# A decoder layer with attention and state-space mixers: VectorE in place of GpSimd, attention's scaling on ScalarE, and the mixers' TensorE instructions ranked 30 places later

## The chip, the cores and the metric

The kernel runs on one core of a Trainium2 chip. The metric is device microseconds of one execution of the whole program. A core has five instruction streams that run side by side and wait for one another by semaphores: TensorE (PE in the profile; its weight loads, PEld, overlap its matmuls), VectorE (DVE), ScalarE (ACT), GpSimd (POOL) and SyncE (SP), which here issues nearly all DMAs. Each stream runs its own instructions in order. An instruction whose input is not there holds all that stand behind it on that engine.

## The reference

One layer of a hybrid decoder, for a prompt of 2048 tokens and for 8 single sample tokens that share its weights. All in fp32, model width 1024, feed-forward width 2816.

```python
h = rms_norm(x, norm1_w)
q, k, v, z, xbc, dt_raw = jnp.split(h @ w_in, SPLIT_IDX, axis=-1)
a = swa_prompt(q, k, v, attn_sinks, rel_bias)        # window 128, 8 heads of 64, 2 kv heads, sinks, bias
s_out, new_conv, new_h = ssm_mixer(z, xbc, dt_raw, conv_buf, h0, ...)   # conv, chunked scan of 128, gate, norm
x = x + jnp.concatenate([a, s_out], axis=-1) @ w_out
h2 = rms_norm(x, norm2_w)
x = x + (jax.nn.silu(h2 @ w_gate) * (h2 @ w_up)) @ w_down
return rms_norm(x, final_norm_w), new_k, new_v, new_conv, new_h
```

The samples do the same with a cache of keys, values, convolution rows and scan state. The kernel returns the outputs and the new caches.

## The kernel before

The tokens are columns, the features partitions. The 16 blocks of 128 tokens and the 8 samples go through in six groups: 2, 3, 3, 3, 3 blocks, and 2 blocks with the samples, so N, the columns of a matmul, is 256, 384 (four times) and 264.

**Split products.** To keep fp32 accuracy, each large product is three passes: both the weight and the activation are split into a hi part (a rounded copy) and a lo part (the value less hi), and `mm3` adds hi by hi, hi by lo and lo by hi. A projection (`proj`) of one unit of 128 outputs is 8 x 3 = 24 matmuls into one of four PSUM banks called psd. The mixers' matmuls and transposes use four others, psm.

**Weights.** `weight` (line 199) gives one half unit. The first uses of a weight load it raw into one of four `wraw` buffers (line 206, on SP), copy it to hi on ACT (207) and subtract on POOL and DVE in turn (lines 208 to 210) for lo. Two steps later the pair is stored to DRAM (214, on SP), at the first, second or third use of the weight, so that a third of the weights is kept at each of the first three groups. From then on the pair is loaded ready-made (203). Five `w2` buffers hold pairs. Loads and stores stand in one queue, SP's.

**Stages of a group.** X (`stage_x`, for the first group `stage_x0`): load, square (ACT), sum (`total`, POOL), reciprocal root (`rinv_b`: one matmul with ones, ACT, DVE) and scaling into hi and lo (`scaled`, lines 333 to 349, whose `low` takes POOL and DVE in turn). A, K, B: the projections of the convolution's inputs, keys and values, queries and gate, with the convolution on DVE and ACT. P: attention, block by block (`attention`, 532). Q: the scan (`ssd`, 704) and its norm. Y: the samples. S: the split of the mixed output (`low`, 919). O: the output projection, with squares and sums for the next norm (`norm_sum`, 950). H: the second norm. F: the feed-forward with `up`, `down`, and hidden parts split by `hid1` and `hid2` (1003 to 1010). Z: the last norm and the output.

**Attention**, in the parts touched: the keys' lo (line 554, POOL), scores on TensorE, a fused bias and maximum on DVE (568), exponentials on ACT (588), the reciprocal of the sum (593, DVE), the scaling of the probabilities by it, four instructions of 128x128 for each key head (603, POOL), transposes (608), hi and lo, a product with the triangle for hi (626, POOL) and for lo (628, DVE), and the product with the values. **The scan**, likewise: the decays are cut to size (738, eight instructions on DVE), and POOL makes the products at 742, 750 and 757.

**The order.** The stages are generators. `run(main, rest)` (1067) steps the main one, a projection at a time, then `tick()`, which issues what `later` has put off, and then a share of each of the others. So the mixers of group i+1 and the first norm of group i+2 are woven into the feed-forward of group i. The program's instructions are issued in this order, each with a rank one higher than the last, and a planner then lays out every engine's stream by the ranks and by its own times: of the instructions it takes to be ready on an engine, the lowest rank comes first. The streams are then fixed.

Of the kernel before, what the change touches and what calls it, by code (L numbers as in the profile page):

```python
# [17 lines left out]
P = 128  # L18
# [10 lines left out]
RH0 = 3  # L29
DM = 1024  # L30
KT = DM // P
NH = 8
# [37 lines left out]


@with_exitstack
def hymba(ctx: ExitStack, tc: tile.TileContext, I: dict, O: dict, groups):
# [26 lines left out]

    V, S, G, PE, SP = nc.vector, nc.scalar, nc.gpsimd, nc.tensor, nc.sync

# [96 lines left out]
    def weight(name, at, w=512):  # L199
        t = T([P, 1024], F32R, tag="w2", bufs=5)[:, :2 * w]  # L200
        hi, lo = t[:, :w], t[:, w:]
        if (name, at) in kept:
            SP.dma_start(t.bitcast(F32), kept[name, at])
            return hi, lo
        raw = T([P, 512], tag="wraw", bufs=4)[:, :w]
        SP.dma_start(raw, I[name][at] if name != "wd" else I[name][:, at:at + w])
        S.activation(hi, raw, AF.Copy)  # L207
        e = G if wn[0] % 2 else V
        wn[0] += 1
        e.tensor_tensor(lo, raw, hi.bitcast(F32), ALU.subtract)  # L210
        k = seen[name, at] = seen.get((name, at), len(seen) % 3) - 1
        if k < 0:
            d = kept[name, at] = DR([P, 2 * w], f"{name}{len(kept)}")
            later(2, lambda: SP.dma_start(d, t.bitcast(F32)))
        return hi, lo
# [65 lines left out]
    def stage_x0(g):  # L281
# [18 lines left out]
        for m in range(KT):  # L300
            G.tensor_tensor(xr[:, m, :N], xr[:, m, :N], xr[:, m, :N], ALU.mult)
            if m:
                V.tensor_tensor(xr[:, 0, :N] if m < KT - 1 else r, xr[:, 0, :N], xr[:, m, :N], ALU.add)
            if m % 4 == 3:
                yield
# [13 lines left out]

    def total(sq, t, N, e=G):  # L320
        e.tensor_tensor(sq[:, :N], sq[:, :N], t[:, :N], ALU.add)  # L321
# [11 lines left out]
    def scaled(x, c, r, N, pair, to):  # L333
# [119 lines left out]
    def stage_k(g):  # L453
# [16 lines left out]
        def rows():  # L470
# [8 lines left out]
            for i, src in enumerate((vf[:, 0:nb], vd[:, :nb])):  # L479
                src = src.rearrange("p b (v c) -> p b v c", v=2)  # L480
                S.activation(vs[:, i, :nb, :, 0:64], src, AF.Copy)
                G.tensor_tensor(vs[:, i, :nb, :, 64:P], src, vs[:, i, :nb, :, 0:64].bitcast(F32), ALU.subtract)
            if last:
# [48 lines left out]
    def attention(g, b):  # L532
# [17 lines left out]
        for kv in range(2):  # L550
            a, o = half[kv], half[1 - kv]
            V.tensor_tensor(qs[o, 4 * kv:4 * kv + 4, :], qT[a, :, tk], qs[a, 4 * kv:4 * kv + 4, :].bitcast(F32), ALU.subtract)
            for r in (a, o):
                G.tensor_tensor(kl[r, kv, :W], kT[a, (b + k0) * P:(b + 2) * P], kh[a, kv, :W].bitcast(F32), ALU.subtract)
        yield
# [44 lines left out]
        def scale(kv):  # L600
            for r in range(4):
                h = kv * 4 + r
                G.tensor_scalar(sc[kv][:, r, 0:P], sc[kv][:, r, 0:P], rd[:, h:h + 1], 1.0, ALU.mult, ALU.mult)

# [11 lines left out]
        def finish(kv):  # L616
# [7 lines left out]
            if not first:  # L624
                own = part(), part()
                G.tensor_tensor(as4(own[0]), as4(f32(ph)), tri4, ALU.mult)
                yield
# [26 lines left out]
    def stage_q(g):  # L654
# [17 lines left out]
        for s0, s1 in ss:  # L672
            G.tensor_tensor(s0[:, :N], s0[:, :N], s1[:, :N], ALU.add)
        yield
# [29 lines left out]
    def ssd(g, b):  # L704
# [36 lines left out]
        xdd = T([P, NH, 64], tag="m2", bufs=M2)  # L741
        G.tensor_tensor(xdd, xdt, sm[:, 1, :].unsqueeze(2).broadcast_to([P, NH, 64]), ALU.mult)
        yo = PS("m")
# [5 lines left out]
        V.tensor_tensor(t1, yo.rearrange("p (a i) -> p a i", a=4), ecs, ALU.mult)  # L749
        G.tensor_tensor(state, state, sm[:, 0, :].unsqueeze(2).broadcast_to([P, NH, 64]), ALU.mult)  # L750
        st = PS("m")
# [3 lines left out]
        for q in range(2):  # L755
            e = csb[:, 4 * q:4 * q + 4, :]
            G.tensor_tensor(e, e, cb[:, q, :].unsqueeze(1).broadcast_to([P, 4, P]), ALU.mult)
        V.tensor_tensor(state, st.rearrange("p (h d) -> p h d", h=NH), state, ALU.add)
# [14 lines left out]
    def stage_y(g):  # L773
# [111 lines left out]
        for i in range(NS):  # L885
# [6 lines left out]
            V.tensor_tensor(f4(xb), bb(bcb, 0), f4(dx[:, 1, :, i:i + 1].broadcast_to([P, 4, P])), ALU.mult)  # L892
            G.tensor_tensor(h, h, dx[:, 0, :, i:i + 1].broadcast_to([P, 4, P]), ALU.mult)
            yield
            G.tensor_tensor(h, h, xb, ALU.add)
            SP.dma_start(O["nss"][:, i], h)
# [15 lines left out]
    def stage_s(g):  # L912
# [6 lines left out]
        def low(t):  # L919
            e = G if t % 2 else V  # L920
            e.tensor_tensor(mix[1][:, t, :N], src[t], mix[0][:, t, :N].bitcast(F32), ALU.subtract)
# [28 lines left out]
    def norm_sum(g, x1, sq, m, N, n=1):  # L950
# [6 lines left out]
        def second():  # L957
            if m:
                total(sq, t[0], N, V if g is gs[-1] and n == 0 else G)
            g["nsq"] = g.get("nsq", 0) + 1  # L960
# [15 lines left out]
    def stage_f(g):  # L976
# [30 lines left out]
        def hid2(f, t, hh, hl):  # L1007
            e = G if f % 2 else V
            e.tensor_tensor(hl[:, 0, :N], t[:, :N], hh[:, 0, :N].bitcast(F32), ALU.subtract)  # L1009
# [57 lines left out]
    def run(main, *rest, units=None, drain=99):  # L1067
# [156 lines left out]
```

## Time and profile before

| what | us |
|---|---|
| three timed runs, median | 2443.29 |
| lowest, highest | 2434.94, 2444.47 |
| the profiled execution | 2437.1 |
| its span, from first to last instruction | 2434.7 |

Mean granted clock of TensorE over the span: 0.985 of full. The chain of work that ended last is put down to TensorE for 68%, to DMA for 7%, to DVE for 2% and to ACT for 1%; the DMA pieces are loads of split weights.

A busy row in the profile gives the time of an engine's instructions, taken together, and their number. A group row gives line, engine, operation, the tiles written and read, partitions x elements, the number, and then the busy us, the mean ns of one, the idle time before them and who ended it. A wait row gives the engine and line that waited, who released it, the us in total, the times, and the longest. A row of the order in time gives start, length, engine, line, operation, tiles and number. The granted clock is the share of the full clock that TensorE was allowed.

### The profile page before, as it was taken

Reading aid. Unit: us, or ns where it says so; the run is one execution under the profiler, and the core shown is the slowest. Engines: PE = TensorE matmul, PEld = TensorE weight load, DVE = VectorE, ACT = ScalarE, POOL = GpSimd, SP = SyncE. Lnnn points to the kernel's source line nnn. Section 1 sums busy time; section 2 is a strip of 40 time slices with the busy share of each in tenths; the row PEclk is TensorE's granted clock in tenths of the full one; section 3 lists DMA queues with packets and bytes.
Section 4 is the critical chain, followed back from the end, with each engine's and each line's share of the span. In section 5 each row is a group of like instructions: output and inputs, shape, how many; then the busy total and the mean of one; then the engine's idle time right before and its main releaser. Section 6 shows DMA issues by size and latency. Waiting matters only on the chain.

```text
span 2434.7 us, 39664 instructions
## 1 busy us (share of the span) xinstructions
PE 2314.5 (95%) x14633; PEld 2244.4 (92%) x14633; DVE 1250.4 (51%) x2526; ACT 875.1 (36%) x1861; POOL 814.4 (33%) x884
## 2 busy tenths in 40 slices
PE   6889898999999999999999999999999999999997
PEld 5779887889999999999999999999989999999997
DVE  8895978564556545344653533453354544233223
ACT  5665556454434434333432422132233212121001
POOL 5555766553444434223322312231123132111000
PEclk9899998999999999999999999999999999999999
DMA  8648575787776777878788887777789788888997
GB/s 276 221 151 284 186 239 195 248 306 272 252 247 212 243 246 278 272 262 277 242 281 285 269 250 243 238 215 240 237 308 301 230 280 270 249 294 306 332 339 259
DMA packets 227227, 628.97 MB, mean 258 GB/s; under 512 B 24323, under 2 KB 57916, under 8 KB 226892
## 3 DMA queue, kind: packets, MB, share of 16 engines
q1 hardware_dynamic: 226892, 626.26, 77.5%
q8 instruction: 116, 1.90, 0.3%
q14 instruction: 75, 0.61, 0.1%
q10 hardware_dynamic: 144, 0.20, 0.0%
HBM read 516.67 MB, written 110.21 MB: 257 GB/s over the span
## 4 chain that ended last, share of the span: by engine, by line
PE 68%; DMA 7%; DVE 2%; ACT 1%; issue 0%; SPq 0%; ACTq 0%; POOL 0%; DVEq 0%
PE psd L104 64%; PE psm L104 4%; DMA w<-wd 2%; DMA w<-wi 2%; DMA w<-wu 1%; DMA w<-wg 1%; DVE x L1042 1%; DVE xr L348 1%; DVE alo L339 0%; DMA out_yT_dram<-x 0%; DMA m<-sbcd 0%; PE psm L608 0%; PE psm L728 0%; DVE w L210 0%; ACT L696 0%
## 5 line engine op out<-in xcount | busy, mean ns | idle before, releaser
L104 PE MATMUL psd<-bhi,w 128*128 128x384 f32 (+1 forms) x4448 | 1097.4, 328 | 40.0 <-DVE w L210 14.9
L104 PEld LDWEIGHTS psd<-bhi,w 128*128 128x128 f32 x4448 | 785.6, 190 | 54.6 <-DVE w L210 19.1
L104 PE MATMUL psd<-blo,w 128*128 128x384 f32 (+1 forms) x2224 | 720.8, 324 | 0.7 <-DVE blo L339 0.6
L104 PE MATMUL psd<-hc,w 128*128 128x384 f32 (+2 forms) x3168 | 527.5, 323 | 28.6 <-DMA w<-wd 9.8
L104 PEld LDWEIGHTS psd<-hc,w 128*128 128x128 f32 x3168 | 502.5, 191 | 43.3 <-issue 12.4
L104 PE MATMUL psd<-ahi,w 128*128 128x384 f32 (+1 forms) x2272 | 516.7, 314 | 22.4 <-DMA w<-wi 8.4
L104 PEld LDWEIGHTS psd<-blo,w 128*128 128x128 f32 x2224 | 423.2, 190 | 2.8 <-DVE blo L339 1.1
L104 PEld LDWEIGHTS psd<-ahi,w 128*128 128x128 f32 x2272 | 386.1, 189 | 31.2 <-DMA w<-wi 5.0
L210 POOL TENSOR_TENSOR w<-wraw,w 128x512 fp32r<-128x512 f32 (+1 forms) x195 | 252.7, 1298 | 382.1 <-ACT w L207 346.3
L104 PE MATMUL psd<-alo,w 128*128 128x384 f32 (+1 forms) x1136 | 354.9, 312 | 0.0
L207 ACT ACTIVATE w<-wraw 128x512 fp32r<-128x512 f32 (+1 forms) x391 | 232.5, 601 | 324.4 <-PE psd L104 187.7
L994 DVE TENSOR_TENSOR x<-psd,x 128x384 f32<-128x384 f32 (+2 forms) x336 | 168.0, 510 | 193.9 <-PE psd L104 193.4
L104 PEld LDWEIGHTS psd<-alo,w 128*128 128x128 f32 x1136 | 215.2, 189 | 1.3
L210 DVE TENSOR_TENSOR w<-wraw,w 128x512 fp32r<-128x512 f32 (+1 forms) x196 | 164.4, 840 | 90.7 <-ACT w L207 88.6
L1009 POOL TENSOR_TENSOR hc<-tmp,hc 128x384 fp32r<-128x384 f32 (+2 forms) x66 | 67.6, 1025 | 356.8 <-ACT hc L1005 356.7
L1001 DVE SCALAR_TENSOR_TENSOR tmp<-tmp,psd 128x384 f32<-128x384 f32 (+2 forms) x132 | 66.7, 505 | 233.2 <-ACT tmp L1015 233.0
L1015 ACT ACTIVATE tmp<-psd 128x384 f32<-128x384 f32 (+2 forms) x132 | 59.7, 452 | 349.4 <-PE psd L104 349.2
L321 POOL TENSOR_TENSOR sq<-sq,tmp 128x384 f32<-128x384 f32 (+2 forms) x112 | 109.7, 979 | 199.4 <-ACT tmp L318 194.4
L1004 DVE SCALAR_TENSOR_TENSOR tmp<-psd,tmp 128x384 f32<-128x384 f32 (+2 forms) x132 | 67.4, 511 | 199.1 <-PE psd L104 198.8
L1005 ACT ACTIVATE hc<-tmp 128x384 fp32r<-128x384 f32 (+2 forms) x132 | 64.4, 488 | 270.4 <-DVE tmp L1004 267.0
L382 DVE SCALAR_TENSOR_TENSOR x<-tmp,cols,x 128x384 f32<-128x384 f32 (+1 forms) x144 | 100.3, 700 | 37.2 <-ACT x L404 26.7
L318 ACT ACTIVATE tmp<-x 128x384 f32<-128x384 f32 (+2 forms) x84 | 40.5, 489 | 137.5 <-DVE x L942 100.4
(269 smaller groups left out, 2145.3 us busy)
## 6 DMA issues: line engine op xcount, KB each, us to landing
w<-wu SPq DMA_DIRECT2D x177, 512.0 KB, 5.0
w<-wg SPq DMA_DIRECT2D x175, 512.0 KB, 4.5
w<-wi SPq DMA_DIRECT2D x144, 512.0 KB, 4.6
w<-wd SPq DMA_DIRECT2D x192, 384.0 KB, 3.8
w<-wo SPq DMA_DIRECT2D x65, 512.0 KB, 4.6
wraw<-in_wg_dram SPq DMA_DIRECT2D x89, 256.0 KB, 4.3
wu<-w SPq DMA_DIRECT2D x44, 512.0 KB, 3.3
wg<-w SPq DMA_DIRECT2D x44, 512.0 KB, 3.7
```

The lines of the kernel that those rows point to most:

```text
L104: PE.matmul(o, l, r, start=start, stop=stop)
L207: S.activation(hi, raw, AF.Copy)
L210: e.tensor_tensor(lo, raw, hi.bitcast(F32), ALU.subtract)
L318: S.activation(t[:, :N], x[:, m, :N], AF.Square)
L321: e.tensor_tensor(sq[:, :N], sq[:, :N], t[:, :N], ALU.add)
L382: V.scalar_tensor_tensor(acc, raw[:, j:j + NP], cwc(j, t), acc, ALU.mult, ALU.add)
L994: V.tensor_tensor(x1[:, m, :N], p[:, :N], x1[:, m, :N], ALU.add)
L1001: V.scalar_tensor_tensor(t[:, :N], t[:, :N], 1.0, pg[:, :N], ALU.add, ALU.mult)
L1004: V.scalar_tensor_tensor(t[:, :N], pu[:, :N], 0.5, t[:, :N], ALU.mult, ALU.mult)
L1005: S.activation(hh[:, 0, :N], t[:, :N], AF.Copy)
L1009: e.tensor_tensor(hl[:, 0, :N], t[:, :N], hh[:, 0, :N].bitcast(F32), ALU.subtract)
L1015: S.activation(t[:, :N], pg[:, :N], AF.Tanh, scale=0.5)
```

## The change

All additions, subtractions and products of two tensors that POOL did go to DVE: the weights' lo (210), the squares of the first norm (301), `total` (321), the lo parts of the norms, of the mix and of the hidden units (339, 921, 1009), those of values and keys (482, 554), the triangle product (626), the norm sums in the scan (673), the scan's three products (742, 750, 757) and the samples' (893, 895). POOL keeps its copies. Attention's scaling (603) becomes an ACT copy with a scale. And the TensorE instructions that `tick()` and the woven-in stages issue within `run`'s main loop are given a rank 30 higher than their place; those of the main stage keep theirs, and nothing is changed in the loop that finishes the rest.

```diff
+PLACES = 30
...
+class Behind:
+
+
+    def __init__(self, tc, engine):
+        self.tc, self.engine, self.places = tc, engine, 0
+
+    def __getattr__(self, op):
+        f = getattr(self.engine, op)
+
+        def issue(*a, **k):
+            rank = self.tc.cur_priority
+            self.tc.cur_priority = rank + self.places
+            f(*a, **k)
+            self.tc.cur_priority -= self.places
+
+        return issue
...
-    V, S, G, PE, SP = nc.vector, nc.scalar, nc.gpsimd, nc.tensor, nc.sync
+    V, S, G, PE, SP = nc.vector, nc.scalar, nc.gpsimd, Behind(tc, nc.tensor), nc.sync
...
-        e = G if wn[0] % 2 else V
-        wn[0] += 1
+        e = V
         e.tensor_tensor(lo, raw, hi.bitcast(F32), ALU.subtract)
...
-            G.tensor_tensor(xr[:, m, :N], xr[:, m, :N], xr[:, m, :N], ALU.mult)
+            V.tensor_tensor(xr[:, m, :N], xr[:, m, :N], xr[:, m, :N], ALU.mult)
...
-    def total(sq, t, N, e=G):
+    def total(sq, t, N, e=V):
...
         def low(m):
-            e = G if m % 2 else V
+            e = V
...
-                G.tensor_scalar(sc[kv][:, r, 0:P], sc[kv][:, r, 0:P], rd[:, h:h + 1], 1.0, ALU.mult, ALU.mult)
+                S.activation(sc[kv][:, r, 0:P], sc[kv][:, r, 0:P], AF.Copy, scale=rd[:, h:h + 1])
...
-            G.tensor_tensor(e, e, cb[:, q, :].unsqueeze(1).broadcast_to([P, 4, P]), ALU.mult)
+            V.tensor_tensor(e, e, cb[:, q, :].unsqueeze(1).broadcast_to([P, 4, P]), ALU.mult)
...
+            PE.places = PLACES
             tick()
             for e in rest:
                 advance(e, e[1])
+            PE.places = 0
```

More of the change, by code (lines that the diff above doesn't have):

```diff
@@ L481, in rows @@
                 S.activation(vs[:, i, :nb, :, 0:64], src, AF.Copy)
-                G.tensor_tensor(vs[:, i, :nb, :, 64:P], src, vs[:, i, :nb, :, 0:64].bitcast(F32), ALU.subtract)
+                V.tensor_tensor(vs[:, i, :nb, :, 64:P], src, vs[:, i, :nb, :, 0:64].bitcast(F32), ALU.subtract)
             if last:
@@ L553, in attention @@
             for r in (a, o):
-                G.tensor_tensor(kl[r, kv, :W], kT[a, (b + k0) * P:(b + 2) * P], kh[a, kv, :W].bitcast(F32), ALU.subtract)
+                V.tensor_tensor(kl[r, kv, :W], kT[a, (b + k0) * P:(b + 2) * P], kh[a, kv, :W].bitcast(F32), ALU.subtract)
         yield
@@ L625, in finish @@
                 own = part(), part()
-                G.tensor_tensor(as4(own[0]), as4(f32(ph)), tri4, ALU.mult)
+                V.tensor_tensor(as4(own[0]), as4(f32(ph)), tri4, ALU.mult)
                 yield
@@ L672, in stage_q @@
         for s0, s1 in ss:
-            G.tensor_tensor(s0[:, :N], s0[:, :N], s1[:, :N], ALU.add)
+            V.tensor_tensor(s0[:, :N], s0[:, :N], s1[:, :N], ALU.add)
         yield
@@ L741, in ssd @@
         xdd = T([P, NH, 64], tag="m2", bufs=M2)
-        G.tensor_tensor(xdd, xdt, sm[:, 1, :].unsqueeze(2).broadcast_to([P, NH, 64]), ALU.mult)
+        V.tensor_tensor(xdd, xdt, sm[:, 1, :].unsqueeze(2).broadcast_to([P, NH, 64]), ALU.mult)
         yo = PS("m")
@@ L749, in ssd @@
         V.tensor_tensor(t1, yo.rearrange("p (a i) -> p a i", a=4), ecs, ALU.mult)
-        G.tensor_tensor(state, state, sm[:, 0, :].unsqueeze(2).broadcast_to([P, NH, 64]), ALU.mult)
+        V.tensor_tensor(state, state, sm[:, 0, :].unsqueeze(2).broadcast_to([P, NH, 64]), ALU.mult)
         st = PS("m")
@@ L892, in stage_y @@
             V.tensor_tensor(f4(xb), bb(bcb, 0), f4(dx[:, 1, :, i:i + 1].broadcast_to([P, 4, P])), ALU.mult)
-            G.tensor_tensor(h, h, dx[:, 0, :, i:i + 1].broadcast_to([P, 4, P]), ALU.mult)
+            V.tensor_tensor(h, h, dx[:, 0, :, i:i + 1].broadcast_to([P, 4, P]), ALU.mult)
             yield
-            G.tensor_tensor(h, h, xb, ALU.add)
+            V.tensor_tensor(h, h, xb, ALU.add)
             SP.dma_start(O["nss"][:, i], h)
@@ L919, in low @@
         def low(t):
-            e = G if t % 2 else V
+            e = V
             e.tensor_tensor(mix[1][:, t, :N], src[t], mix[0][:, t, :N].bitcast(F32), ALU.subtract)
@@ L958, in second @@
             if m:
-                total(sq, t[0], N, V if g is gs[-1] and n == 0 else G)
+                total(sq, t[0], N, V)
             g["nsq"] = g.get("nsq", 0) + 1
@@ L1007, in hid2 @@
         def hid2(f, t, hh, hl):
-            e = G if f % 2 else V
+            e = V
             e.tensor_tensor(hl[:, 0, :N], t[:, :N], hh[:, 0, :N].bitcast(F32), ALU.subtract)
```

## The prediction

> **What bounds the kernel now.** I read the page first, then the busy time by stretches, then the waits of TensorE in the stretch where it loses most. All sums are made against the profiled execution, 2437.1 us (its span of 2434.7 and 2.4 around it).
>
> ```profile
> PE 2314.5 (95%) x14633; PEld 2244.4 (92%) x14633; DVE 1250.4 (51%) x2526; ACT 875.1 (36%) x1861; POOL 814.4 (33%) x884
> ```
>
> ```profile
> 0.00:549.00 549.00, 474.79 (x3259) 438.98 (x3260) 410.90 (x775) 308.59 (x660) 318.41 (x331) 0.95 0.70 234
> 549.00:1769.00 1220.00, 1211.23 (x7110) 1191.95 (x7110) 589.36 (x1191) 431.28 (x896) 380.54 (x415) 1.00 0.77 252
> 1769.00:2196.00 427.00, 414.58 (x2598) 405.81 (x2597) 184.78 (x415) 102.29 (x237) 100.06 (x120) 0.99 0.85 278
> 2196.00:2434.70 238.70, 213.90 (x1671) 207.63 (x1670) 65.35 (x148) 32.95 (x70) 15.38 (x18) 0.98 0.88 310
> ```
>
> The columns of the second fence are the stretch, its length, then busy time (and instructions) of PE, PEld, DVE, ACT and POOL, the granted clock, the DMA share and GB/s. TensorE is the bound: 95% busy. Its idle time is length less busy: 74.2 us in the first 549 us, 8.8 in the next 1220, 12.4 up to 2196, and 24.8 at the end, where DMA moves 310 GB/s. A change to element-wise engines can only give back idle time of TensorE, and 62% of that lies in the first 549 us. There the granted clock is 0.95, so up to another 0.05 x 549 = 27 us go to a slower clock. DVE is 75% busy there and POOL 58%.
>
> ```profile
> PE psd L104 <- DVE w L210: 15.6, 14, 3.1
> PE psd L104 <- ACT w L207: 10.4, 10, 2.6
> PE psd L104 <- POOL w L210: 8.5, 12, 1.7
> PE psd L104 <- DVE x L994: 8.3, 5, 2.5
> PE psd L104 <- DVE wdt L292: 6.3, 1, 6.3
> PE psd L104 <- ACT ahi L345: 4.8, 1, 4.8
> PE psm L104 <- DVE dt L261: 4.3, 2, 4.0
> ...
> PE psm L104 <- DVE m L622: 1.6, 2, 1.4
> ...
> PE psm L608 <- POOL big L603: 1.4, 3, 0.7
> ```
>
> These are TensorE's waits up to 549 us: total, times, longest. They are mostly for the split of a weight into hi (ACT, L207) and lo (POOL or DVE, L210), and for DVE chains. The DMA queue waits for the same split, as the next rows show, in which SPq is the queue, L206 the load of a raw weight and L214 the store of a split one:
>
> ```profile
> SPq L206 <- POOL w L210: 81.2, 53, 7.0
> SPq L206 <- DVE w L210: 76.4, 31, 8.2
> SPq L214 <- POOL w L210: 41.3, 27, 4.0
> ```
>
> A raw load needs one of four `wraw` buffers, and these come free when lo is done. So early on the loop load, hi, lo, next load limits TensorE.
>
> **DVE and POOL slow each other.** The same DVE instructions, beside a working POOL and beside an idle one, in order of time:
>
> ```profile
> 247.96 1.86 POOL L554 TENSOR_TENSOR m<-kT,m 64x256 fp32r<-64x256 f32 x2
> 250.87 2.50 POOL L210 TENSOR_TENSOR w<-wraw,w 128x512 fp32r<-128x512 f32 x2
> ```
>
> ```profile
> 248.36 5.87 DVE L738 TENSOR_SCALAR big<-big,cs 128x128 f32<-128x128 f32 x8
> 381.63 8.69 DVE L348 SCALAR_TENSOR_TENSOR xr<-xr,cols,sq 128x384 f32<-128x384 f32 x8
> 1036.62 1.68 DVE L348 SCALAR_TENSOR_TENSOR tmp<-x,cols,sq 128x384 f32<-128x384 f32 x3
> 1103.69 0.68 DVE L210 TENSOR_TENSOR w<-wraw,w 128x512 fp32r<-128x512 f32 x1
> 1104.29 2.14 DVE L738 TENSOR_SCALAR big<-big,cs 128x128 f32<-128x128 f32 x8
> ```
>
> ```profile
> 1107.66 1.30 POOL L757 TENSOR_TENSOR big<-big,m 128x512 f32<-128x512 f32 x1 [7.11 <-ACT big L747]
> ```
>
> At 248 us POOL works beside L738, and eight take 5.87 us. At 1104 us POOL has been idle since 1100.6, and the same eight take 2.14 (0.27 each against 0.73). L348 takes 1.09 in the early run of eight and 0.56 at 1036 us. Take POOL's work away, and DVE's own instructions shrink.
>
> **The change, part by part.** Prices of what moves, from the groups kept apart by form:
>
> ```profile
> L210 POOL TENSOR_TENSOR w<-wraw,w 128x512 fp32r<-128x512 f32 x147 | 200.7, 1368 | 311.8 <-ACT w L207 287.5 <-DMA w<-wg 6.8 <-DMA wg<-w 5.3
> ...
> L603 POOL TENSOR_SCALAR big<-big,sm 128x128 f32<-128x128 f32 x128 | 53.5, 436 | 102.6 <-DVE sm L593 84.3 <-ACT w L207 12.0 <-ACT ssm L730 6.3
> ...
> L403 POOL COPY tmp<-hist 128x3 f32<-128x3 f32 x48 | 14.9, 315 | 5.2 <-DVE tmp L701 3.0 <-DVE x L393 2.1
> L407 POOL COPY hist<-tmp 128x3 f32<-128x3 f32 x48 | 13.1, 274 | 102.0 <-ACT tmp L402 86.3 <-DVE tmp L400 15.4
> ```
>
> ```profile
> L210 DVE TENSOR_TENSOR w<-wraw,w 128x512 fp32r<-128x512 f32 x148 | 122.7, 830 | 75.5 <-ACT w L207 73.9 <-DMA wu<-w 0.2 <-DMA wg<-w 0.2
> ...
> L738 DVE TENSOR_SCALAR big<-big,cs 128x128 f32<-128x128 f32 x128 | 51.4, 470 | 1.3 <-ACT m L720 1.2
> ```
>
> *POOL to DVE.* POOL holds 814.4 us. Its scaling (53.5) goes to ACT, and its small copies stay, some 32 us (14.9 + 13.1, and a few more). Some 729 us move. L210 is the largest group: 1.37 us on POOL, 0.83 on DVE now, 0.68 with POOL quiet, a ratio of 0.50; on that ratio DVE gains about 365 us. DVE's own work falls: 148 x (0.83 - 0.68) = 22 for L210, 128 x (0.47 - 0.27) = 26 for L738, and the other instructions with their inputs in SBUF likewise; I take 150 in all, an estimate from these two and from L348. DVE then has some 1465 us, 60% of the span. In the first 549 us it has 410.9 now; POOL's 318 there less scaling and copies is about 290, so 145 come in. Own savings I put at 90, as POOL is densest there. That makes about 465, or 85% of the stretch as it stands. The sum is close to one engine's capacity, but it does not break it.
>
> What becomes shorter is latency. A split's lo takes 0.68 us in place of a mean of 1.1, the buffer comes free earlier, and the DVE runs that block others shrink. TensorE's 74.2 us of early idle time are 6.3 of the start (L292), 10.4 + 4.8 = 15.2 on ACT, and some 53 that are nearly all on DVE or POOL. Of the 53 I take half: 26. Of the 15.2, which follow the raw loads and, at L345, DVE's L348, I take a third: 5. Bounds: nothing, if the DVE queue eats it, and all 68. The nearest rows, L210 at 0.83 against 0.68 and L348 at 1.09 against 0.56, save a fifth and a half; I stay nearer to the upper because POOL's 1.37 falls to 0.68 too.
>
> Against this, line 301's eight squares at the start leave POOL for DVE, eight at some 0.4 us (the half-width share of 0.68 and more): 3 us on DVE before line 306's sum, of which I charge 1.
>
> *The clock.* Stretches, with the same columns as above:
>
> ```profile
> 183.00:244.00 61.00, 59.30 (x413) 58.49 (x411) 31.92 (x51) 35.68 (x71) 33.35 (x31) 1.00 0.82 282
> 244.00:305.00 61.00, 54.13 (x413) 48.90 (x412) 55.84 (x105) 32.68 (x76) 46.38 (x42) 1.00 0.58 190
> 366.00:427.00 61.00, 49.68 (x341) 45.49 (x341) 50.91 (x84) 36.02 (x69) 37.56 (x37) 0.89 0.61 198
> ```
>
> The clock is whole where TensorE idles 1.7 us of 61 and 0.89 where it idles 11.3; but it is whole too at 244, with 6.9 us idle. So it answers to long idleness, not to each wait. I take 5 of the 27 us; bounds 0 and 20.
>
> The Trainium skill, "TensorE: Matmul & The Clock Gate", section "Part 1: The HAM clock gate (the "warmup" mystery)", says that the clock halves after an idle window of about 3.4 us and is whole again after a busy one. By it waits of one or two microseconds cost no clock, so the term would be near 0 if only those go, and a few us if the 4.8 us wait for L345 goes. The rows at 244 and 366 bear it out.
>
> *Later stages.* A chain of waits at 784 us shows DVE holding the DMA queue:
>
> ```profile
> 784.46 6.53 DVE xr L348 x8
> ...
> 797.92 7.64 DMA w<-wd
> ```
>
> The store L214 waits for a lo that stands behind these runs on DVE, and weight loads stand behind the store on SP. With quiet POOL L348's run is 8 x 0.56 = 4.5. TensorE's idle time there is small: of the 8.8 us I take 4, and 2 of the 12.4 after it. The last 24.8 beside 310 GB/s I leave.
>
> *Scaling on ACT.* Nearest rows:
>
> ```profile
> L297 ACT ACTIVATE bhi<-xr,cols 128x256 fp32r<-128x256 f32 x8 | 3.4, 497 | 1.1 <-DMA xr<-in_xT_dram 1.1
> L730 ACT ACTIVATE ssm<-ssm 128x16 f32<-128x16 f32 x16 | 3.4, 212 | 26.4 <-DVE ssm L724 26.4
> ```
>
> A 128x128 with a scale lies between 0.21 and 0.50; I take 0.35, so 45 us more on an engine 36% busy, and four in a row hold ACT 1.4 us. Each waits for the reciprocal (L593); behind it on ACT stand the hi parts (L207) and the gate's tanh (L1015), for which TensorE waits. ACT's idle 44% of the early stretch hides it: 0, with a bound of 16 blocks x 1.4 = 22 lost, and 1.4 gained (L608's wait).
>
> *Ranks.* Thirty places are about one projection (24 matmuls and its few other instructions), 4.2 us by a row of the chain of waits:
>
> ```profile
> 641.40 4.18 PE psd L104 x24
> ```
>
> TensorE is held by mixer instructions (psm) only 7.3 us by the rows shown of the first stretch (4.3 + 1.6 + 1.4), within the sum already. The mixers end one projection later, and the mixers' other engines move with it; projections of the next group lie between them and the output projection. Cost 0; bounds 5 us gained, and 4.2 lost at each of the two places with little between, groups 0 and 5. No DMA carries a new rank.
>
> **Sum:** -26 - 5 + 1 - 5 - 4 - 2 = -41, so 2437.1 - 41 = 2396. The three timed runs (2434.9 to 2444.5) have a median of 2443.3, 6 above the profiled one; I put the median some 4 above the sum: **2400**.
>
> **Rivals.**
>
> *DVE becomes the bound early (slower).* Before, two engines shared the lo parts; now each stands in one queue behind L738 or L348, and the DMA queue's stores behind it. At 244-305 DVE is already 92% busy. If its own instructions keep their present lengths, the 290 us of POOL cost at 0.83/1.37 = 0.61 another 177, and the early stretch needs 411 + 177 = 588 us, 39 more than it has; with TensorE's losses on top, 2437 + 39 = 2476 or more. It decides when DVE saves under 60 us of its own there (588 less 60 is 528, 96% of 549). Against it speak the pairs 0.27/0.73 and 0.56/1.09. Chance 0.12.
>
> The Trainium skill, "Perfetto Trace Analysis", section "Optimizing Scalar/DVE Operations", advises moving work off a saturated DVE, even to POOL, though it adds that the two share a read port, so that it may not help. Its first half speaks for this rival, its second for my sum; the paired rows are on the second's side.
>
> *The raw loads bound it (no difference).* The row of the page's DMA issues gives a raw load's KB and its us from issue to landing:
>
> ```profile
> wraw<-in_wg_dram SPq DMA_DIRECT2D x89, 256.0 KB, 4.3
> ```
>
> If the loop is mostly this landing, the split's 0.4 us hardly counts: a tenth of the loop. Then the early waits on DVE and POOL fall by 5, the later ones by 2: 2430, by the median 2433. For it speaks the wait of ACT on raw weights; against it, that SP itself waits 81.2 + 76.4 us for lo before it can load. Chance 0.16.
>
> *The ranks take back what the splits give.* They should keep TensorE from waiting for mixer inputs, but only 7.3 us of such waits stand there early; if instead the output projection waits for a mix that ends one projection later, at each of six groups, 6 x 4.2 = 25 us come on top: 2396 + 25 + 4 = 2425. For it: a mixer step waits for the one before it. Against it: in the 1220 us after 549 TensorE idles 8.8 us in all, so the mixers are not late now. Chance 0.06.
>
> **How the numbers follow.** My case has 0.66, and its own range is 2355 (all 68 us, 8 of the clock and the later 6) to 2425. Faster by over 0.5%, about what a measurement here can tell from no change, is below 2431: 0.66, the 0.06, and an eighth of the raw-load case, together 0.74. Slower, above 2455: 0.12. Between: 0.14. The range from 2352 to 2440 leaves out the slow case and a little at the bottom.
>
> **What would show it.** Right: L738 near 0.27 and L348 near 0.56 throughout; DVE near 1465 us; POOL near 32; TensorE's idle time in the first group's stages down by 30 us; SP's waits for L210 well below 157 us. Wrong: DVE over 95% in the early slices with L210 on DVE the first of TensorE's waits and longer than 15.6 + 8.5; new psm waits, or output projections that wait for the mix; a clock below 0.95 early.

## The result and the profile after

| | before | after |
|---|---|---|
| median, us (lowest to highest) | 2443.88 (2434.94 to 2446.01) | 2406.02 (2402.79 to 2410.51) |
| runs | 4 | 4 |
| profiled execution, us | 2437.1 | 2406.6 |
| its span, us | 2434.7 | 2404.8 |

The ratio is 0.9853, with a 95% interval of 0.9824 to 0.9883: 1.5% faster. The forecast was 2400.

First the rows that the page and the stretches have for the changed kernel: busy time of each engine, mean granted clock, and the same four stretches as before with busy time of PE, PEld, DVE, ACT and POOL, clock, DMA share and GB/s.

```profile
PE 2319.7 (96%) x14633; PEld 2243.0 (93%) x14633; DVE 1383.6 (58%) x3173; ACT 911.4 (38%) x1989; POOL 33.3 (1%) x109
```

```profile
core 0: 2404.8 us, clock 0.990
```

```profile
0.00:549.00 549.00, 501.74 (x3497) 474.32 (x3498) 439.24 (x1056) 334.33 (x729) 17.12 (x55) 0.97 0.76 255
549.00:1769.00 1220.00, 1216.03 (x7077) 1181.27 (x7075) 677.17 (x1497) 451.78 (x970) 12.48 (x41) 1.00 0.76 250
1769.00:2196.00 427.00, 416.94 (x2601) 408.04 (x2602) 208.17 (x483) 101.86 (x240) 3.66 (x13) 1.00 0.83 277
2196.00:2404.80 208.80, 185.03 (x1462) 179.36 (x1461) 59.02 (x139) 23.42 (x53) 0.00 (x0) 0.97 0.89 314
```

Two things are to be read here. TensorE's idle time, span less busy, fell from 120.2 to 85.1 us, and 26.9 of these 35.1 us went in the first stretch (74.2 to 47.3). But its busy time did not fall with the better clock (0.985 to 0.990): it rose, from 2314.5 to 2319.7 us, with the same 14633 matmuls. Something makes the same matmuls dearer. That is what the experiments are about.

The waits of TensorE in the first 549 us (total, times, longest), and of the DMA queue there; L226 and L228 are the split's hi and lo, L225 the load of a raw weight, L232 the store of a split one:

```profile
PE psd L85 <- ACT w L226: 9.1, 12, 1.6
PE psd L85 <- DVE tmp L381: 7.6, 1, 7.6
PE psd L85 <- DVE w L228: 6.9, 8, 2.4
```

```profile
SPq L225 <- DVE w L228: 107.6, 82, 6.3
SPq L232 <- DVE w L228: 76.8, 35, 8.3
```

TensorE's waits for the lo of a weight were 15.6 on DVE and 8.5 on POOL; 6.9 are left. The queue's waits for it before a raw load fell from 157.6 (81.2 + 76.4) to 107.6 us; those before a store rose, from 58.1 (41.3 on POOL and 16.8 on DVE) to 76.8.

The groups of DVE's instructions by shape (number, busy us, mean ns, idle before), with L756 for the old L738 and L366 for L348, and one early run of eight of each in the order in time:

```profile
L228 DVE TENSOR_TENSOR w<-wraw,w 128x512 fp32r<-128x512 f32 x295 | 200.5, 686 | 86.2 <-ACT w L226 83.1
L756 DVE TENSOR_SCALAR big<-big,cs 128x128 f32<-128x128 f32 x128 | 34.7, 340 | 0.0
L366 DVE SCALAR_TENSOR_TENSOR xr<-xr,cols,sq 128x384 f32<-128x384 f32 x32 | 17.4, 611 | 0.1
```

```profile
225.34 2.13 DVE L756 TENSOR_SCALAR big<-big,cs 128x128 f32<-128x128 f32 x8
354.09 4.32 DVE L366 SCALAR_TENSOR_TENSOR xr<-xr,cols,sq 128x384 f32<-128x384 f32 x8
```

Eight take 2.13 and 4.32 us where they took 5.87 and 8.69 in before. POOL's busy time fell by 781 us (814.4 to 33.3). Attention's scaling went to ACT, the rest to DVE, and DVE is busy only 133 us longer.

### The profile page after: what moved, and what is told of

It is laid out like the page before. It is cut to its first block, busy times and chain, and to the rows that moved or that the text cites. A ratio compares the mean times of both kernels' runs of the same rounds, so it can differ in the third digit from the quotient of the medians.

```text
span 2404.8 us, 39251 instructions
## 1 busy us (share of the span) xinstructions
PE 2319.7 (96%) x14633; PEld 2243.0 (93%) x14633; DVE 1383.6 (58%) x3173; ACT 911.4 (38%) x1989; POOL 33.3 (1%) x109
## 4 chain that ended last, share of the span: by engine, by line
PE 72%; DMA 6%; DVE 1%; ACT 1%; issue 0%; SPq 0%; ACTq 0%; DVEq 0%
PE psd L85 67%; PE psm L85 5%; DMA w<-wd 2%; DMA w<-wi 2%; DMA w<-wg 1%; DMA out_yT_dram<-x 1%; DMA w<-wu 1%; DVE x L1060 0%; DMA w<-wo 0%; DMA m<-sbcd 0%; ACT L714 0%; ACT big L606 0%; SPq L957 0%; DVE tmp L717 0%; ACT L711 0%
## 5 line engine op out<-in xcount | busy, mean ns | idle before, releaser
L85 PE MATMUL psd<-hc,w 128*128 128x384 f32 (+2 forms) x3168 | 543.2, 324 | 17.2 <-DMA w<-wd 6.0
L226 ACT ACTIVATE w<-wraw 128x512 fp32r<-128x512 f32 (+1 forms) x391 | 232.7, 602 | 316.6 <-PE psd L85 206.5
L228 DVE TENSOR_TENSOR w<-wraw,w 128x512 fp32r<-128x512 f32 (+1 forms) x391 | 252.5, 653 | 101.6 <-ACT w L226 98.1
L400 DVE SCALAR_TENSOR_TENSOR x<-tmp,cols,x 128x384 f32<-128x384 f32 (+1 forms) x144 | 80.0, 567 | 34.0 <-ACT x L422 22.9
L1027 DVE TENSOR_TENSOR hc<-tmp,hc 128x384 fp32r<-128x384 f32 (+2 forms) x132 | 67.3, 510 | 29.8 <-ACT hc L1023 29.5
L339 DVE TENSOR_TENSOR sq<-sq,tmp 128x384 f32<-128x384 f32 (+2 forms) x119 | 61.4, 516 | 31.2 <-ACT tmp L336 30.0
L586 DVE CUSTOM_DVE_ANT_0 big<-psm,bias 128x256 f32<-128x256 f32 (+1 forms) x128 | 47.7, 411 | 47.5 <-PE psm L85 47.4
```

Of the source, the lines that this page charges most:

```text
L85: f(*a, **k)
L400: V.scalar_tensor_tensor(acc, raw[:, j:j + NP], cwc(j, t), acc, ALU.mult, ALU.add)
L586: V.tensor_tensor_reduce(sc[h // 4][:, h % 4 + i, :W], ps[:, i * 256:i * 256 + W], bias[:, h + i, k0 * P:], 1.0, NEG, ALU.add, ALU.max, m[ ...
```

## The experiments

Of the theories in the expectations, A is that each passage of TensorE between a projection and a mixer instruction costs time, F that only a passage behind a full fp32 instruction does; their rival is that mixers 30 places late make others wait. P is that DVE's instructions suffer from POOL's use of SBUF's ports, and S that the weights' split is all of the gain. Each run is timed beside before on the same chip; the ratios have that run's own before.

**1. The ranks.** First the change without its ranks, then the ranks alone, put into the kernel before.

```diff
-PLACES = 30
+PLACES = 0
```

> The changed kernel with the ranks set to 0; the engines stay as changed. Theory P (POOL's absence brings the whole gain, and the ranks cost a part of it: in the woven feed-forwards TensorE passes between projection and mixer instructions four times as often, and there the changed kernel gives back some 12 of the 42 us it had won by 518 us): about 2394 us, at or below the changed kernel's 2406, with the lead over the kernel before kept at about 42 us to the end. Theory R (the ranks bring an essential part of the gain, by keeping TensorE from waiting for mixer inputs early): 2420 us or more, with new early waits of psm instructions.

```diff
 (before)
+PLACES = 30
+class Behind: ...
-    V, S, G, PE, SP = nc.vector, nc.scalar, nc.gpsimd, nc.tensor, nc.sync
+    V, S, G, PE, SP = nc.vector, nc.scalar, nc.gpsimd, Behind(tc, nc.tensor), nc.sync
```

> The kernel before with the ranks alone. Theory P: no gain, 2444 to 2462 us, since TensorE alternates more often. Theory R: 2420 to 2435 us.

| kernel | median, us | ratio to before | interval |
|---|---|---|---|
| without the ranks | 2375.8 | 0.9745 | 0.9730 to 0.9759 |
| ranks alone | 2462.9 | 1.0103 | 1.0085 to 1.0121 |

The page's busy row of the two, without the ranks first:

```profile
PE 2288.4 (96%) x14633; PEld 2228.2 (94%) x14633; DVE 1383.1 (58%) x3173; ACT 912.0 (38%) x1989; POOL 29.9 (1%) x109
```

```profile
PE 2343.5 (95%) x14633; PEld 2258.1 (92%) x14633; DVE 1252.3 (51%) x2526; ACT 877.9 (36%) x1863; POOL 813.2 (33%) x884
```

```profile
core 0: 2372.6 us, clock 0.995
```

The last row is the clock without the ranks. The ranks lose 30 us in one setting (2406.0 less 2375.8) and 24 in the other (2462.9 less the 2438.8 of before beside it); the other edits gain 63 (2438.8 less 2375.8). Theory P had the direction in both, but put the kernel without the ranks at 2394, 18 us too high. And the loss is busy time: with the ranks TensorE is busy 31.3 us longer in the one pair (2319.7 against 2288.4) and 29.0 in the other (2343.5 against 2314.5), while its idle time hardly differs in the first pair (85.1 and 2372.6 - 2288.4 = 84.2).

**2. Passage or lateness.** The same distance ahead instead of behind: the mixers are early, so nothing waits for them longer, but they are as finely mixed with the projections. Then 400 places behind.

```diff
-PLACES = 30
+PLACES = -30
```

> The changed kernel with the ranks at 30 places earlier in place of 30 later. In the planned order TensorE passes from projection to mixer instructions 540 times (557 in the changed kernel, 250 without ranks, 251 before), but the mixers are not late. Theory A (each passage costs TensorE about 0.1 us, (2406 - 2376) / 307): about 2404 us. Rival L (it is the mixers' lateness that costs 30 us): 2376 us or less.

```diff
-PLACES = 30
+PLACES = 400
```

> The changed kernel with the ranks at 400 places later. The mixers are far later, but the planned order has only 289 passages. Theory A: 2376 + 39 x 0.1 = 2380 us, give or take 6. Rival L: more than the changed kernel's 2406 us.

Counted in TensorE's order in time: how often a projection's matmul (psd) is followed by a mixer instruction (psm).

| kernel | passages | median, us | ratio (interval) |
|---|---|---|---|
| before | 251 | 2443.9 | |
| no ranks | 250 | 2375.8 | 0.9745 (0.9730 to 0.9759) |
| 30 behind (after) | 557 | 2406.0 | 0.9853 (0.9824 to 0.9883) |
| 30 ahead | 540 | 2409.5 | 0.9879 (0.9851 to 0.9907) |
| 400 behind | 289 | 2534.8 | 1.0402 (1.0370 to 1.0434) |

Thirty ahead costs as much as thirty behind, and again in busy time (2321.7 us against 2288.4), so at this distance the cost isn't lateness. Without ranks the mixers' instructions stand in clusters where the planner finds them ready; a rank moved by a fixed distance makes single ones alternate with the projections' matmuls. The last row, though, was a miss: few passages should have given about 2380. At 400 places lateness does cost, as the waits of TensorE over the whole span show:

```profile
PE psd L85 <- ACT bhi L363: 16.9, 4, 7.9
PE psm L85 <- DVE tmp L691: 15.8, 2, 13.5
PE psd L85 <- DVE tmp L1019: 13.8, 7, 6.6
```

```profile
core 0: 2530.5 us, clock 0.965
```

Projections there wait for the split of a norm and for the feed-forward's elementwise work, the scan's norm waits for a sum, and the clock falls: TensorE idles 181.8 us (2530.5 less 2348.7 busy), where it idled 84.2 without the ranks. So there are two costs, each with its own distance.

**3. Which passages.** The mixers' instructions are of two types: the scores and the products with the values read rounded operands (fp32r, as the projections do), the transposes, decays and products with the state read full fp32. The rank is moved for one type at a time:

```diff
         def issue(*a, **k):
-            rank = self.tc.cur_priority
-            self.tc.cur_priority = rank + self.places
+            n = self.places if a[1].dtype == F32R else 0
+            self.tc.cur_priority += n
             f(*a, **k)
-            self.tc.cur_priority -= self.places
+            self.tc.cur_priority -= n
```

> The changed kernel with the 30 places given only to those mixer matmuls whose weights are of type fp32r (scores, and the product with the values); the fp32 ones and all transposes keep their place. The planned order has 385 passages from mixer to projection instructions, 250 without ranks; the 135 more are after fp32r. Theory A (any passage costs 0.1 us): 2376 + 13 = 2389 us. Theory F (only a projection matmul behind an fp32 mixer instruction is late, 0.26 to 0.35 us where 0.17 is usual and 0.18 behind an fp32r one): 2374 to 2382 us.

The other kernel has `!=` in the place of `==`.

> The counterpart: the 30 places only for the fp32 mixer matmuls and the transposes. 395 planned passages, of which some 120 more than without ranks are after fp32. Theory A: 2376 + 14 = 2390 us. Theory F: 74 more behind transposes and the like at 0.09 and 47 more behind the scan's last product at 0.18, and that product itself 0.1 longer behind a projection: 2376 + 7 + 13 = 2396 us, and more than 12 us above its counterpart.

| moved | passages | median, us | ratio (interval) |
|---|---|---|---|
| fp32r only | 385 | 2380.2 | 0.9756 (0.9737 to 0.9774) |
| full fp32 only | 395 | 2400.8 | 0.9843 (0.9824 to 0.9861) |

Nearly the same number of passages, 4 us over the kernel without ranks in one case and 25 in the other. The 4 can't be told from nothing, as the intervals overlap; the busy times say the same, 2288.2 us for the first, 2316.4 for the second and 2288.4 without ranks. Theory A missed with the first. Theory F's numbers came near (2374 to 2382, and 2396), but one of its two prices is wrong, as the traces show. The order in time of TensorE (start, length, tiles, number) for the second kernel, at a place where transposes alternate with projections:

```profile
652.73 0.51 PE L85 MATMUL psd<-bhi,w 128*128 128x384 f32 x2
653.08 0.27 PE L85 MATMUL psm<-cst,big 128*128 128x128 f32 x1
653.10 0.42 PE L85 MATMUL psd<-blo,w 128*128 128x384 f32 x1
653.36 0.27 PE L85 MATMUL psm<-cst,big 128*128 128x128 f32 x1
653.39 0.42 PE L85 MATMUL psd<-bhi,w 128*128 128x384 f32 x1
653.65 0.27 PE L85 MATMUL psm<-cst,big 128*128 128x128 f32 x1
```

and for the first, where the transposes of the same part stand together:

```profile
651.65 0.51 PE L85 MATMUL psd<-bhi,w 128*128 128x384 f32 x2
652.00 0.34 PE L85 MATMUL psd<-blo,w 128*128 128x384 f32 x1
652.17 0.34 PE L85 MATMUL psd<-bhi,w 128*128 128x384 f32 x1
652.34 0.60 PE L85 MATMUL psm<-cst,big 128*128 128x128 f32 x4
```

Read the starts, not the lengths. Among projections one matmul starts 0.17 us after another (652.00 to 652.17). Behind a transpose a projection's matmul takes from 653.10 to 653.36, 0.26 us, but the transpose itself only 0.02 (653.08 to 653.10). The two together take 0.28 us. Where the transposes stand together, one takes 0.11 us ((0.60 - 0.27) / 3 in the last row) and a projection's matmul 0.17, which is 0.28 too: a single transpose between projections costs nothing. The changed kernel has attention's scores, of the fp32r type, between projections, and the next start comes 0.18 us after that of the projection's matmul (607.24 to 607.42):

```profile
607.12 0.28 PE L85 MATMUL psm<-m,big 128*128 128x256 f32 x1
607.24 0.34 PE L85 MATMUL psd<-bhi,w 128*128 128x384 f32 x1
607.42 0.28 PE L85 MATMUL psm<-m,big 128*128 128x256 f32 x1
607.53 0.34 PE L85 MATMUL psd<-blo,w 128*128 128x384 f32 x1
```

The whole sum, from the starts of all matmuls behind the 2700th (about 420 us in), each counted to the next start, by the bank that it and the one before it wrote; starts over 0.6 us apart are put apart as waits:

| | without ranks: number, us | with ranks: number, us | difference |
|---|---|---|---|
| projection behind projection | 10835, 1757.5 | 10550, 1714.5 | -43.0 |
| projection behind mixer | 169, 43.8 | 454, 110.3 | +66.5 |
| mixer behind projection | 169, 24.6 | 455, 57.9 | +33.3 |
| mixer behind mixer | 731, 82.5 | 445, 51.6 | -30.9 |
| waits | 28, 33.8 | 28, 37.1 | +3.3 |

The first four rows come to +25.9 us for 285 passages more, 91 ns each. Before the 2700th matmul the spacings other than waits are 6.8 us longer with the ranks; there are 22 passages more there, and the clock is 0.97 and not 0.98. The two together are 32.7, against 31.3 of busy time.

The 91 ns are a mean, not the price of each passage. To divide the 25.9 us, charge each mixer instruction with its own time to the next start and, where a projection stands behind it, with what that projection takes over 162 ns, the mean between projections. With the ranks the scan's last product (176 instructions, full fp32, 64 outputs each) then costs 18.9 us more, the scores and the products with the values (fp32r) 2.5, all transposes 0.9 and the rest 0.5; 3.1 lie between projections. The scan's last product stands out in the other kernels as well: 18.3 us more where only full fp32 was moved, 23.8 with 30 places ahead, 19.0 with the ranks alone (against before), and 1 less where only fp32r was moved. Its rows without the ranks, and with them:

```profile
623.34 1.09 PE L85 MATMUL psm<-big,m 128*64 128x128 f32 x16
624.36 0.44 PE L85 MATMUL psd<-hc,w 128*128 128x384 f32 x1
```

```profile
635.31 0.44 PE L85 MATMUL psd<-hc,w 128*128 128x384 f32 x1
635.68 0.43 PE L85 MATMUL psm<-big,m 128*64 128x128 f32 x2
636.04 0.44 PE L85 MATMUL psd<-hc,w 128*128 128x384 f32 x1
```

Sixteen of its instructions in a row take 1.02 us (623.34 to 624.36), 0.13 for two. Two that the ranks left by themselves take 0.36 (635.68 to 636.04). In a row they mostly start two at a time, under 20 ns apart: 118 such pairs in the whole execution without the ranks, 74 with them. Why two that stand alone don't start together was not followed. So most of what the ranks cost is this one product taken apart. No run moves the ranks of everything but this product, so its share rests on the traces alone.

**4. POOL's work.** The split of the weights alone on DVE, in the kernel before; and everything except that split:

```diff
 (before)
-        e = G if wn[0] % 2 else V
-        wn[0] += 1
+        e = V
```

> The kernel before with only the weights' lo parts all on DVE; the rest of POOL's work stays on POOL, no ranks. Theory P, by the port: POOL loses 253 of its 814 us, so DVE's own instructions shrink by a part only, and DVE also gets the work: some 2430 us. Rival S (the split loop alone was what held TensorE early): 2405 to 2410 us, all of the gain.

```diff
 (after, PLACES = 0)
-        e = V
+        e = G if wn[0] % 2 else V
+        wn[0] += 1
```

> The changed kernel without ranks, but with the weights' lo parts on POOL and DVE in turn, as before. Theory P: some of the gain is lost, 2405 to 2420 us, and L738's counterpart lies between 0.27 and 0.47 us a piece. Rival S: nearly all of the gain is lost, 2435 us or more. Rival N (the split may be on either engine, only DVE's chains count): 2394 us, as without ranks.

The first gives 2404.9 (ratio 0.9859, 0.9844 to 0.9874), the second 2404.8 (0.9857, 0.9840 to 0.9873). Each half is worth 34 us and both together 63: they nearly add. The theory that the split brings little more than its own waits, at about 2430, missed; the rival's number (2405 to 2410) was met but for 0.1 us, though not its reason, that the split is the whole gain. For the second kernel theory P's 2405 to 2420 was met but for 0.2 us, with the decays' instructions at 389 ns, and its two rivals missed. DVE's groups in the first kernel, where POOL is still busy 579 us with the other work:

```profile
L209 DVE TENSOR_TENSOR w<-wraw,w 128x512 fp32r<-128x512 f32 x295 | 219.6, 750 | 105.4 <-ACT w L207 102.6
L737 DVE TENSOR_SCALAR big<-big,cs 128x128 f32<-128x128 f32 x128 | 42.9, 404 | 1.2 <-ACT m L719 1.0
L347 DVE SCALAR_TENSOR_TENSOR xr<-xr,cols,sq 128x384 f32<-128x384 f32 x32 | 26.8, 903 | 0.0
```

They lie between the means of before (830, 470 and 1014 ns) and of after (686, 340 and 611), as POOL's busy time does.

**5. What POOL does, or that it is busy.** Two kernels without the ranks get POOL work that nobody needs at each split of a weight: in the first it reads, in the second it only writes.

```diff
+        scr = T([P, 64], tag="scr")
+        for _ in range(4):
+            G.tensor_tensor(scr, cst[:, 0:64], cst[:, 64:128], ALU.mult)
```

> The changed kernel without ranks, and beside each weight's split four products of 128x64 on POOL that read two constant tiles and write a scratch tile that nobody reads. Theory P (a POOL that reads SBUF slows DVE's instructions, whoever needs its result): L738's counterpart rises above 0.27 us a piece, and the time by 10 to 40 us over 2376. Rival D (POOL's absence helped only because its slow results no longer stand in the chains): 2376 us, and DVE's instructions stay as they are.

```diff
+        scr = T([P, 64], tag="scr")
+        for _ in range(8):
+            G.memset(scr, 0.0)
```

> As the run before, but POOL writes the scratch tile eight times (memset of 128x64) and reads nothing. By the Trainium skill's rule that a DVE instruction with two SBUF inputs contends with a GpSimd instruction that reads SBUF, not with one that only writes: 2376 us, and DVE's instructions with two inputs as without POOL. Rival W (any POOL access blocks): slower, with DVE's instructions longer. Theory D: 2376 us.

Medians 2499.9 (ratio 1.0254, 1.0228 to 1.0280) with reads and 2377.5 (0.9747, 0.9720 to 0.9773) with writes. Groups with reads:

```profile
L229 DVE TENSOR_TENSOR w<-wraw,w 128x512 fp32r<-128x512 f32 x295 | 214.2, 732 | 80.6 <-ACT w L227 77.5 <-PE psd L85 0.5
L759 DVE TENSOR_SCALAR big<-big,cs 128x128 f32<-128x128 f32 x128 | 41.9, 394 | 0.1
```

```profile
L231 POOL TENSOR_TENSOR scr<-cst 128x64 f32<-128x64 f32 x1564 | 696.6, 445 | 121.8 <-DMA cst<-in_consts_dram 3.1
```

and with writes:

```profile
L229 DVE TENSOR_TENSOR w<-wraw,w 128x512 fp32r<-128x512 f32 x295 | 200.7, 686 | 88.0 <-ACT w L227 84.9 <-DMA w<-wg 0.2
L759 DVE TENSOR_SCALAR big<-big,cs 128x128 f32<-128x128 f32 x128 | 34.6, 340 | 0.1
```

```profile
L231 POOL MEMSET scr<- 128x64 f32 x3128 | 476.9, 152 | 176.7 <-POOLq L1236 0.3
```

Beside 697 us of POOL instructions that read, the split takes 732 ns; beside 477 us of those that only write, 686, as beside an idle POOL. The traces also tell which of these instructions ran while POOL was busy. Mean ns where POOL was busy for half of the instruction's time or more, and where it was idle throughout, with their numbers:

| kernel | split, 128x512 | decays, 128x128 | norm's scaling, 128x384 |
|---|---|---|---|
| before | 1047 (53), 688 (73) | 890 (31), 336 (96) | 1224 (21), 611 (9) |
| POOL reads | 747 (221), 688 (74) | 449 (64), 339 (64) | 673 (16), 610 (16) |
| POOL only writes | 685 (206), 688 (87) | 340 (64), 340 (64) | 609 (16), 612 (16) |

Beside an idle POOL they take the same in all three, and the same as in the changed kernel (686, 340 and 611). So it is POOL's reading that lengthens DVE's instructions, while it lasts. The Trainium skill, "SBUF — State Buffer", section "Who interferes with whom", says that a DVE instruction with two SBUF inputs contends with a GpSimd instruction that reads SBUF and not with one that only writes it; by that rule the split suffers from the one and not from the other, and the two rows for it agree. The decays' instruction reads one tensor and a column of scalars; the reads lengthened it as well (394 ns against 340), which that rule does not cover.

The 124 us between the kernel with reads and the same without POOL work aren't the price of the port alone. DVE waits there for a copy of the convolution that stands behind the useless instructions in POOL's queue:

```profile
DVE x L403 <- POOL tmp L424: 94.6, 16, 55.3
```

With the shorter writes this wait is down to 2.3 us. So the pair shows the mechanism by the durations, and its times don't give its price. The forecast for the reads, 10 to 40 us over 2376, missed.

**6. Two small parts.** Both without the ranks: the first norm's squares (line 301 of before) back on POOL, and attention's scaling back on POOL.

```diff
-            V.tensor_tensor(xr[:, m, :N], xr[:, m, :N], xr[:, m, :N], ALU.mult)
+            G.tensor_tensor(xr[:, m, :N], xr[:, m, :N], xr[:, m, :N], ALU.mult)
```

> The changed kernel without ranks, and the eight squares of the first norm back on POOL. The prediction charged 1 us for them, of 3 us of DVE work; TensorE's longest early wait, 7.9 us for the first use of that norm, says more. If the squares make that wait: 2371 to 2374 us, with the wait down to 2 to 5 us. If DVE's other work makes it: 2376 us.

```diff
-                S.activation(sc[kv][:, r, 0:P], sc[kv][:, r, 0:P], AF.Copy, scale=rd[:, h:h + 1])
+                G.tensor_scalar(sc[kv][:, r, 0:P], sc[kv][:, r, 0:P], rd[:, h:h + 1], 1.0, ALU.mult, ALU.mult)
```

> The changed kernel without ranks, and attention's scaling back on POOL. The prediction put its move to ACT at 0. Theory P: POOL reads SBUF again for 53 us of 814 (about 1/15 of the engines' 63 us): 2376 to 2382 us. If ACT pays for it (bound 22 us): 2355 to 2373 us.

Squares on POOL: 2379.5 (0.9753, 0.9737 to 0.9769). Scaling on POOL: 2381.1 (0.9762, 0.9743 to 0.9782). Both intervals overlap that of the kernel without ranks, so neither part can be told from nothing; both forecasts for the squares (2371 to 2374, and 2376) lie below the measured time. With the squares on POOL, TensorE's wait for the first norm does shrink, from the first row (no ranks) to the second:

```profile
PE psd L85 <- DVE tmp L381: 7.9, 1, 7.9
```

```profile
PE psd L85 <- DVE tmp L381: 1.9, 1, 1.9
```

but those 6 us don't come out as time; where they go was not followed.

## Why the prediction came out

The time was in the range and within 6 us of the point, and the reason is only half the one given: two terms of the sum were wrong by about 20 and 30 us, and they had opposite signs. The point also has 4 us on top of the sum, because the timed runs of before lay above its profiled execution; those of the changed kernel do not (2406.0 against 2406.6), so against the sum itself, 2396, the profiled time is 10 us off. That the total came so near is luck.

| term | predicted, us | measured, us | by |
|---|---|---|---|
| idle time of TensorE | -36 (-26 -5 +1 -4 -2) | -36.0 without ranks, -35.1 with | span less busy |
| busy time, from the engines' part | -5 | -26.1 | 2288.4 against 2314.5 |
| busy time, from the ranks | 0 | +31.3 | 2319.7 against 2288.4 |
| sum | -41 | -30 | profiled executions |

- **Early waits: right.** POOL's absence shortened DVE's instructions as foreseen: 0.27 us each in the run of L738 where 0.27 was named, 0.54 in that of L348 where 0.56 was. In the first 549 us 26.9 us of idle time went; the terms for that stretch had 30.
- **DVE's load: right in kind.** DVE is busy 1383.6 us where 1465 were forecast. Added up by their lengths, group by group, the instructions that moved cost DVE 371 us (365 were forecast), and its old ones give back 193 (150 were taken); lengths that overlap on DVE count once in the busy time, which makes up the rest. The rival in which it becomes the bound didn't come: it is busy 439.2 of the first 549 us, 80%. The rival of the raw loads didn't come either; the split is worth 34 us by itself.
- **The clock: the term was mis-sized.** It was put at 5 of 27 us with the reason that the clock answers to long idleness, not to each wait. It answers to shorter waits than that. In before, the stretches of 42 to 45.5 us and of the 6.5 us behind it (columns as above, the clock is the third number from the end), and a matmul in the first with its wait:

```profile
42.00:45.50 3.50, 1.37 (x10) 1.24 (x10) 3.29 (x12) 1.24 (x3) 1.47 (x2) 1.00 0.50 188
45.50:52.00 6.50, 6.20 (x28) 5.68 (x28) 4.75 (x13) 2.94 (x7) 2.63 (x5) 0.50 0.78 234
```

```profile
44.13 0.51 PE L104 MATMUL psd<-bhi,w 128*128 128x256 f32 x2 [2.21 <-DVE w L210]
```

A wait of 2.2 us, with TensorE busy 1.37 us of 3.5, is followed by 6.5 us at half clock, in which it is busy 6.2. But not every wait of this length has that behind it. This one, 11 us earlier and longer, has full clock before and behind:

```profile
33.23 0.51 PE L104 MATMUL psd<-bhi,w 128*128 128x256 f32 x2 [2.77 <-DVE w L210]
```

What decides can be read from the fourteen traces together. In all of them the clock changes only on a grid of 3.41 us. Of the grid's stretches at full clock, from 20 us on, all 112 in which TensorE was busy under 44% were followed by half clock, none of the 9183 over 70%, and 35 of the 265 between. The wait of 2.2 us fell into one stretch, busy 41%; that of 2.77 us lay across two, busy 49 and 60%. So a short wait costs clock only where its stretch of the grid is left less than about half busy, and there it can cost more than itself. Once the waits go, the clock of the first 549 us is 0.99 without the ranks, 0.97 with them. The Trainium skill, "TensorE: Matmul & The Clock Gate", section "Part 1: The HAM clock gate (the "warmup" mystery)", has the clock halve after an idle window of about 3.4 us; here a shorter idle time was enough, and the measurement decides. How much of the 26 us is clock has two readings: by the mean clock, 0.015 x 2434.7 - 0.005 x 2372.6 = 24.7; by the spacings of matmuls other than waits, 15.9 less up to the 2700th and 2.8 behind it.

- **The ranks: the step that failed.** They were priced at 0 with bounds of 5 gained and 8 lost, since only waits and lateness were looked at: would something come later than it is needed? The cost is in the matmuls themselves, 31.3 us of busy time; by the spacings some 19 of them are the scan's last product, whose instructions take longer apart than in a row. The rival "the ranks take back what the splits give" had the size, 25 us, but by an output projection waiting for a late mix; 30 places ahead, which makes nothing late, cost the same, so it isn't that.
- **Scaling on ACT: right.** 128 instructions took 392 ns each (0.35 was the estimate), 39.3 us in all:

```profile
L621 ACT ACTIVATE big<-big,sm 128x128 f32<-128x128 f32 x128 | 39.3, 392 | 5.1 <-DVE sm L611 4.9
```

Back on POOL it is no faster, so the cover held.
- **The squares of line 301** were to cost 1 us; the wait they lengthen is 6 us longer, but the time of the two kernels can't be told apart.

What stays open: how the 63 us divide between DVE's shorter instructions and the shorter chain of a split that no longer changes engines. The run that was to price the first had a queue of its own in the way.

The best of the kernels run is the change without its ranks: 2375.8 us, 2.5% under before.

## What to carry to other kernels

When an edit changes the order of work on the engine that sets the time, look at what the new order takes apart, not only at who waits for whom: idle time was the same here and 30 us went in busy time, most of it in one product whose instructions no longer stood in a row. To price a passage, take both instructions together: behind a transpose the projection looked 0.09 us dearer, and the transpose was that much cheaper. Small waits of a bounding TensorE can cost more than their length, where they leave a stretch of the clock's grid less than about half busy. And a total that fits is no proof of its terms: only the run without the ranks showed that two of them were wrong.

## What the runs showed of the hardware

- A projection's fp32r matmul of 384 columns takes 0.17 us to the next start behind its like, 0.18 behind attention's fp32r scores and 0.26 behind a full fp32 transpose; but transpose and projection together take 0.28 us whether they alternate or not.
- Sixteen full fp32 matmuls of 64 outputs take 1.02 us in a row, most starting two at a time; two of them between projections take 0.36.
- The granted clock changes on a grid of 3.41 us. It was halved behind every stretch in which TensorE was busy under 44% (112 of 112, in fourteen traces), and never behind one over 70%.
- A DVE instruction is longer while POOL reads SBUF: beside the work that POOL had in before, 1047 ns and not 688 for a split, 890 and not 336 for the decays. Beside POOL's memsets nothing changes (685 and 340).
- POOL's busy time fell by 781 us, and all of it but the scaling (39.3 us on ACT) cost DVE 133 us of busy time.
